# Weights prepared one product earlier: the order of weight casts, block factors and late loads in a two-layer mixer trunk

## The chip, the core and the metric

The kernel runs on one core of a Trainium2 chip. TensorE multiplies matrices, VectorE and ScalarE do elementwise work, GpSimd (POOL) and SyncE (SP) mostly issue DMAs here. The metric is the device time of one execution in microseconds.

## What is computed

Two layers over 2048 tokens of 1024 features. Cut to what matters:

```python
for l in range(2):
    shift, scale, gate = split(silu(c) @ w_ada[l] + b_ada[l], 3)
    h = rms_norm(x, g_pre[l]) * (1 + scale) + shift
    u_a, b_a, c_a, gate_a, u_p, gate_p = split(h @ w_in[l], 6)
    y_a = b_a * causal_conv3(c_a * u_a, w_conv[l]) * silu(gate_a)
    y_p = pool(u_p, w_pool[l], pool_scale[l]) * silu(gate_p)  # windows 2, 4, 8, 16
    y = concat([y_a, y_p]) @ w_out[l]
    x = x + gate * rms_norm(y, g_post[l])
```

All tensors are float32.

## The kernel before, in words

Features lie on the partitions, in chunks of 128 (k = 0 to 7); tokens go in two blocks of 1024, each in two halves of 512. Every float32 operand of a large product is split into a high part, rounded by a cast, and a low part, source less high part; a product is made of three passes (high·high, high·low, low·high), each a matmul of 128x128 weights with 128x512 data.

The work is a row of phases, for layer and block (0,0), (0,1), (1,0), (1,1): an in-phase (h times w_in, and the mixer, into y), then an out-phase (y times w_out, evicted to DRAM as ysp, with the sums of its squares), in which the operands h of the next block are also made. The block factor ry, one over the root of the mean square of y times w_out, comes after the out-phase, in the first stretch of the next in-phase: `opening(p)` evicts the last column chunk (p = 0), splits the sums of squares (`mean_split`, p = 1), and at p = 3 sums them over the partitions by two matmuls a half (`mean_mm`) and makes the factors: logarithm and exponential on ScalarE, each behind a load of its table, then three Newton steps on VectorE (L278 to L280). Tasks in the background (`Paced`) use ry to finish the block: ysp times ry, plus x, to x1 or to the output.

In layer 0 an in-phase takes 24 column groups with all 8 chunks each. In layer 1 `in_seven` multiplies by Winograd's form of Strassen's scheme: two column groups, two halves of k and two halves of the tokens form a 2x2 block product in 7 products of 12 matmuls instead of 8. Twelve pairs of column groups give 84 products. Four of the seven weight operands are sums, split beforehand and loaded from DRAM ready (512 KB, POOL's queue, L714); three are raw quarters (256 KB, SP's queue) that ScalarE casts (L729) and VectorE settles, that is subtracts for the low part (L739). They lie in a ring of seven slots. The sums of data blocks of h come from the out-phase, twelve "late" ones (L1038, split at L183 and L186) in the first products. After each product, ScalarE or VectorE takes its result from PSUM (L828 to L860).

```python
    LOAD, HIGH, SETTLE = 6, 3, 2
...
            for p, (_, hn) in enumerate(PRODUCTS):
                m = 7 * n + p
                load(m + 1 + LOAD)
...
                if final and p in closing:
                    free -= closing[p](kept)
                free -= settle(m + 1 + SETTLE)
                high(m + 1 + HIGH)
```

So weights are loaded six products ahead, cast three and settled two ahead. In the last pair `closing[p]` brings y back from DRAM (`yin`, loaded at L884 into six landing buffers) in 14 pieces of 128x512, splits them for the out-phase, and loads and settles the first weights of the out-phase, whose class `Weights` has the same three steps (cast L209, settle L219). In the in-phases and the out-phases those weights share three slots in turn.

Each engine runs its instructions in the order in which they stand in the program (`manual_schedule`), and so do the queues of SP and POOL: an instruction that waits holds all behind it on its engine. The places of tiles (`ring`, `wplaces`, `yorder`) are lists of slot numbers; a tile in a slot waits for the last reader of the tile that lay there.

## Time and profile before

| | |
|---|---|
| runs of the kernel | 1442.15, 1446.51, 1449.56 us, median 1446.51 |
| the profiled execution | 1441.82 us |
| its span in the trace | 1440.0 us |
| mean granted TensorE clock | 0.986 of full speed |
| in-phase (0,0) and start | to 318.4 us |
| out-phase, in-phase, out-phase of (0,0) to (0,1) | to 763.6 us |
| in-phase (1,0), 84 products | 763.6 to 1008.3 us |
| out-phase (1,0) | to 1095.5 us |
| in-phase (1,1), 84 products | to 1335.0 us |
| last out-phase | to the end |

How to read it: an engine's busy time counts only its own instructions, so TensorE at 97% leaves 48 us in which it stands. A row of the timeline gives the start, the time that the run of like instructions took, their number, and in brackets how long the engine stood before and which instruction released it. The granted clock is 1.00 at 2.4 GHz and 0.50 at 1.2 GHz.

### The profile page before, as it was taken

To read this page: it belongs to the slowest core of one execution; us is meant where nothing else is said; L and a number is where in the kernel's file an instruction comes from. 1 tells how busy PE (TensorE), PEld (TensorE's weight loads), DVE (VectorE), ACT (ScalarE), POOL (GpSimd) and SP (SyncE) were. 2 spreads that over 40 slices of the span, in tenths; PEclk is the share of its full clock that TensorE was granted. 3 is DMA by queue.
4 is the path that set the end of the run, shared out by engine and by line. 5 is a ranking of instruction groups with operands and counts; after the bars stand their busy time and mean duration, and the time that the engine had idled before them with its cause. 6 is when DMAs were issued, how large, how long until landed. Compare 5 with 4: busy or idle time off the path is not lost. (4 is left out here: it accounts for less than half of the span.)

```text
span 1440.0 us, 17843 instructions
## 1 busy us (share of the span) xinstructions
PE 1391.7 (97%) x6244; PEld 1142.8 (79%) x6244; DVE 932.5 (65%) x1519; ACT 500.9 (35%) x869; POOL 256.9 (18%) x372
## 2 busy tenths in 40 slices
PE   8889999999999999999997999999998999999996
PEld 4678888878888888888885888887886888887796
DVE  7962778755445575775855766768765655658455
ACT  4332334444443222224646222123645111113421
POOL 4601123310011111210121222210122122121000
PEclk9999999999999999999999999999999999999998
DMA  8405678635446656654567888887458677877422
GB/s 309 182 0 180 236 242 292 215 140 181 137 146 204 220 184 204 212 169 138 199 210 239 247 244 254 270 245 255 151 194 285 208 229 231 240 237 240 143 88 88
DMA packets 143116, 291.23 MB, mean 202 GB/s; under 512 B 15921, under 2 KB 32305, under 8 KB 143026
## 3 DMA queue, kind: packets, MB, share of 16 engines
q1 hardware_dynamic: 96338, 171.58, 36.4%
q0 software_dynamic: 46688, 118.51, 25.2%
q8 instruction: 49, 0.80, 0.2%
q14 instruction: 41, 0.34, 0.1%
HBM read 217.67 MB, written 72.35 MB: 201 GB/s over the span
## 5 line engine op out<-in xcount | busy, mean ns | idle before, releaser
L804 PE MATMUL ps_in<-h,ws 128*128 128x512 f32 x2016 | 464.6, 392 | 16.6 <-DVE ws L739 15.1
L804 PEld LDWEIGHTS ps_in<-h,ws 128*128 128x128 f32 x2016 | 379.9, 189 | 100.5 <-DVE ws L739 19.7
L390 PE MATMUL ps_in<-h,ws 128*128 128x512 f32 x1968 | 450.6, 390 | 0.0
L390 PEld LDWEIGHTS ps_in<-h,ws 128*128 128x128 f32 x1968 | 368.7, 188 | 76.0
L390 PE MATMUL ps_out<-y,ws 128*128 128x512 f32 (+1 forms) x1728 | 353.7, 367 | 2.2 <-ACT ws L209 2.0
L390 PEld LDWEIGHTS ps_out<-y,ws 128*128 128x128 f32 x1728 | 298.7, 189 | 56.6 <-ACT ws L209 2.9
L209 ACT CAST ws<-raw 128x512 fp32r<-128x512 f32 x146 | 89.6, 622 | 300.5 <-PE ps_in L390 144.9
L219 DVE TENSOR_TENSOR ws<-raw,ws 128x512 fp32r<-128x512 f32 x146 | 99.6, 688 | 115.8 <-ACT ws L209 112.8
L390 PE MATMUL ps_in<-h,w 128*128 128x512 f32 x336 | 86.8, 418 | 14.3 <-ACT h L379 7.2
L714 POOL DMA_DIRECT2D ws<-sums x96 | 67.5, 704 | 185.4 <-PE ps_in L804 171.8
L390 PEld LDWEIGHTS ps_in<-h,w 128*128 128x128 f32 x336 | 66.8, 201 | 33.6 <-ACT h L379 9.6
L987 POOL DMA_DIRECT2D ysp<-yg x48 | 26.1, 544 | 269.9 <-ACT yg L986 269.7
L828 ACT COPY v<-ps_in 128x512 f32<-128x512 f32 x24 | 14.1, 589 | 167.3 <-PE ps_in L804 167.3
L739 DVE TENSOR_TENSOR ws<-raw,ws 128x512 fp32r<-128x512 f32 x72 | 49.3, 685 | 17.6 <-ACT ws L729 17.6
L729 ACT CAST ws<-raw 128x512 fp32r<-128x512 f32 x72 | 41.5, 620 | 24.0 <-PE ps_out L390 17.7
L263 DVE SCALAR_TENSOR_TENSOR adaw<-adaw,cb 128x512 f32<-128x512 f32 x64 | 42.8, 685 | 10.7 <-DMA adaw<-wada 9.0
L849 ACT ACTIVATE second<-second 128x1024 f32<-128x1024 f32 x16 | 17.0, 1062 | 93.1 <-DVE second L843 90.2
L995 DVE TENSOR_TENSOR acc<-acc,sq 128x512 f32<-128x512 f32 x42 | 28.9, 692 | 24.9 <-ACT sq L992 24.9
L473 POOL DMA_DIRECT2D sums<-s13h x24 | 18.0, 748 | 147.3 <-ACT s13h L465 123.1
L843 DVE TENSOR_TENSOR second<-ps_in,v 128x512 f32<-128x512 f32 x16 | 11.1, 692 | 44.4 <-PE ps_in L804 44.4
L1083 POOL DMA_DIRECT2D x<-fin x32 | 18.8, 586 | 116.6 <-DVE fin L1078 113.8
L1076 DVE TENSOR_TENSOR fin<-fin,ry 128x512 f32<-128x512 f32 x48 | 32.8, 684 | 6.0 <-DMA fin<-ysp 6.0
(178 smaller groups left out, 1322.5 us busy)
## 6 DMA issues: line engine op xcount, KB each, us to landing
ws<-sums POOLq DMA_DIRECT2D x96, 512.0 KB, 7.1
raw<-win SPq DMA_DIRECT2D x122, 256.0 KB, 4.4
adaw<-wada SPq DMA_DIRECT2D x64, 256.0 KB, 4.5
raw<-wout SPq DMA_DIRECT2D x64, 256.0 KB, 3.3
sums<-raw POOLq DMA_DIRECT2D x48, 256.0 KB, 5.0
ysp<-yg POOLq DMA_DIRECT2D x48, 256.0 KB, 3.7
fin<-ysp SPq DMA_DIRECT2D x48, 256.0 KB, 4.9
raw<-win SPq DMA_DIRECT2D x80, 128.0 KB, 4.5
```

The lines of the kernel that those rows point to most:

```text
L209: nc.scalar.copy(self.ws[m][:, 0], self.raws[m].rearrange("p (a b) -> p a b", b=P))
L219: nc.vector.tensor_tensor(t[:, 1], raw, t[:, 0].bitcast(F32), op=ALU.subtract)
L263: nc.vector.scalar_tensor_tensor(w[n], w[n], 1.0, cb[:, n * HS : (n + 1) * HS], op0=ALU.mult, op1=ALU.mult, accum_out=m[:, l, j : j + 1])
L390: nc.tensor.matmul(ps[s], lhsT=ws[k // KH][:, wi, k % KH, :], rhs=rhs(k, ri, s), start=first and (wi, ri) == PASSES[0], stop=last and (wi, ...
L714: nc.gpsimd.dma_start(ops[m].rearrange("p a b c -> p a (b c)"), sums[l, n][:, :, SUM[a]])
L729: nc.scalar.copy(ops[m][:, 0], raws[m].rearrange("p (a b) -> p a b", b=P))
L739: nc.vector.tensor_tensor(ops[m][:, 1], raw, ops[m][:, 0].bitcast(F32), op=ALU.subtract)
L804: nc.tensor.matmul(ps, lhsT=ops[m][:, wi, k, :], rhs=h[hn][k][:, ri, :], start=p < 4 and k == 0 and (wi, ri) == (0, 0), stop=k == KH - 1 a ...
L987: nc.gpsimd.dma_start(ysp[l, b][:, j, s * HS : (s + 1) * HS], t)
L995: tt(accs[s], accs[s], q, op=ALU.add)
L1076: nc.vector.tensor_tensor(e[0], e[0], ry[l, b, s], op=ALU.mult)
L1083: nc.gpsimd.dma_start(x1[b][:, k, s * HS : (s + 1) * HS], e[1])
```

## The change

Six edits in the order of the work; no arithmetic is changed.

- `in_phase` takes the weights of the out-phase behind it (`nxt`) and casts, loads and settles the first of them between the matmuls of its last product; the background work is paced to end four steps sooner.
- In `in_seven` the settle and the cast stand right behind a product's matmuls, ahead of the opening, of the closing and of what takes the product's result; they are for products three and four ahead.
- The ring begins with the slots that come free first: `turned` and `wplaces[1:] ... wplaces[:1]`.
- `opening` sums the squares and begins both factors at p = 2, behind one table load that serves logarithm and exponential (`log_exp`, which moves from the head of the out-phase to its norm and to p = 2), and ends them at p = 3 and p = 4. There are 13 table loads in the program instead of 19.
- `closing` begins at the last product of the pair before the last and goes in threes: y is loaded two products before its split. The first out weights are loaded at p = 2 and p = 4 and settled at p = 3 and p = 4.
- `out_last` takes its weights' raw parts from the three buffers of `w`, not from the six landings, and casts before it loads, half by half.

```diff
-    def in_phase(l, b, hrhs, tasks, later, started, yplaces, wplaces, ws=None, opening=None):
+    def in_phase(l, b, hrhs, tasks, later, started, yplaces, wplaces, nxt, ws=None, opening=None):
...
                         ws.settle(2)
-        bg = Paced(tasks, 1, KT * (len(order) - first) - (10 if started else 20))
+        bg = Paced(tasks, 1, KT * (len(order) - first) - (10 if started else 24))
         for n in range(first, len(order)):
...
                 turn = KT * (n - first) + k
-                if opening and turn in (0, 4, 9):
-                    opening((0, 1, 3)[(0, 4, 9).index(turn)])
+                if n == len(order) - 1 and k > KH:
+                    if k == KH + 1:
+                        nxt.high(2)
+                        nxt.load(3)
+                    else:
+                        free -= nxt.settle(k - KH - 1)
+                if opening and turn in OPENING:
+                    opening(OPENING.index(turn))
                     free = 0
                 free = work.run(free)
-                if not opening or turn > 9:
+                if not opening or turn > OPENING[-1]:
                     bg.run(free + 1 if free > 0 else 0)
...
+    OPENING = (0, 4, 9, 11, 13)
+
     def in_weights(l, order, first, places):
...
     SUM = {"S1": 0, "S2": 1, "S3": 2, "S4": 3}
-    LOAD, HIGH, SETTLE = 6, 3, 2
+    LOAD, HIGH, SETTLE = 6, 4, 3
...
                 later.tick()
-                free = 2.5
+                free = 2.5 - settle(m + 1 + SETTLE)
+                high(m + 1 + HIGH)
                 if n == 0:
...
                         bg.prime(1)
-                if final and p in closing:
-                    free -= closing[p](kept)
-                free -= settle(m + 1 + SETTLE)
-                high(m + 1 + HIGH)
                 if p == 0:
...
                     free -= E2
+                at = p if final else p - 7 if n == len(PAIRS) - 2 else None
+                if at == -1:
+                    bg.drain()
+                if at in closing:
+                    free -= closing[at](kept)
                 free = mix.run(free)
-                if (n or p > 3) and n < len(PAIRS) - 1:
+                if (n or p > 4) and n < len(PAIRS) - 1 and at != -1:
                     bg.run(max(free, 0.1))
-                if n == len(PAIRS) - 2 and p == 6:
-                    bg.drain()
         mix.drain()
...
-        log_exp()
         h = {name: [None] * KH for name in EARLY + LATE}
...
         def norm():
+            log_exp()
             for s in range(NH):
...
                 st["parts"] = [mean_split(accs.pop(s)) for s in range(NH)]
-            if p == 3:
-                st["mean"] = [mean_mm(parts) for parts in st["parts"]]
+            if p == 2:
+                log_exp()
                 for s in range(NH):
-                    ry[l, b, s] = rsqrt_short(st["mean"][s], HS, half("ry"))
+                    ry[l, b, s] = half("ry")
+                    st[s] = rsqrt_steps(mean_mm(st["parts"][s]), HS, ry[l, b, s])
+                    next(st[s])
+            if p in (3, 4):
+                for _ in st[p - 3]:
+                    pass
...
             for j in range(KT):
-                if part == 0 and j:
-                    ws.load(2 * j + 6)
-                    ws.high(2 * j + 3)
                 ps = bank("ps_out")[:, :n]
                 for i, k in enumerate(OUT_ORDER if part or j == 0 else range(KT)):
+                    if part == 0 and i % KH == 0:
+                        ws.high(2 * j + i // KH + 3)
+                        ws.load(2 * j + i // KH + 5)
                     if part == 0 and i % KH == 1:
...
+    turned = lambda places, n: places[n % 3 :] + places[: n % 3]
+
     def between(many, few):
...
             tasks += [call_task(lambda: load_wpool(1), 0.1)]
-            y = in_phase(0, 0, hrhs, tasks, later, started, yplaces, wplaces)
+            ws = out_weights(0, turned(wplaces, 34))
+            y = in_phase(0, 0, hrhs, tasks, later, started, yplaces, wplaces, ws)
     with working(8, 6, 4, 3, 0), tc.manual_schedule():
-        ws = out_weights(0, wplaces)
-        ws.load(3)
-        ws.settle(2)
-        first = in_weights(0, IN_ORDER, 0, wplaces[1:] + wplaces[:1])
+        first = in_weights(0, IN_ORDER, 0, turned(ws.places, 16))
         hrhs, _, opening = out_phase(0, 0, y, 0, 1, ws, hplaces, None, first)
...
         tasks = between(mixes, fins[:4]) + between(between(adas, sums_), fins[4:])
-        y = in_phase(0, 1, hrhs, tasks, later, None, yplaces, first.places, first, opening)
+        ws = out_weights(0, first.places)
+        y = in_phase(0, 1, hrhs, tasks, later, None, yplaces, first.places, ws, first, opening)
     wplaces = first.places
     with working(5, 8, 6, 3, 2), tc.manual_schedule():
-        ws = out_weights(0, wplaces)
-        ws.load(3)
-        ws.settle(2)
         for n, (l, b) in enumerate(blocks[2:], 2):
...
             h, fills, opening = out_phase(*blocks[n - 1], y, l, b, ws, hplaces, lplaces)
-            ring = wplaces[:2] + yorder[:4] + wplaces[2:3]
+            ring = wplaces[1:] + yorder[:4] + wplaces[:1]
             hp = {}
...
             if last:
-                ws = out_weights(l, after + late_places[:9], lambda: landing("raw"))
+                ws = out_weights(l, after + late_places[:9])
             else:
...
                 def f(kept):
-                    if p == 0:
-                        for q in inner[:4]:
-                            y_load(*q)
-                        ws.load(1)
-                        return 0
-                    for q in inner[4 * p - 4 : 4 * p]:
+                    for q in inner[max(0, 3 * p - 3) : max(0, 3 * p)]:
                         y_settle(*q, kept)
-                    for q in inner[4 * p : 4 * p + 4]:
+                    for q in inner[3 * p + 3 : 3 * p + 6]:
                         y_load(*q)
-                    return 2.8 + (ws.settle(p - 2) if p > 2 else 0)
+                    if p == 2:
+                        ws.load(2)
+                    if p == 4:
+                        ws.load(3)
+                    return 2.1 * (p > 0) + (ws.settle(p - 2) if p in (3, 4) else 0)
...
-            closing = {p: close(p) for p in range(5)}
+            closing = {p: close(p) for p in range(-1, 6)}
             kept = in_seven(l, b, h, fills, opening, tasks, later, old, closing)
```

What it moves, at three places.

ScalarE at the opening of in-phase (1,0), before: `ws<-raw` is the cast of a weight, `ah` and `late` are the statistics' and the operands' high parts, `rs_a`, `rs_v`, `ry` the factors.

```order
L729 CAST ws<-raw 128x512 x2
L286 ACT_TABLE_LOAD
L286 ACTIVATE rs_a<-ps_stat,epsc 128x512
L287 ACTIVATE rs_v<-ps_stat,epsc 128x512
L288 ACT_TABLE_LOAD
L288 ACTIVATE ry<-rs_a 128x512
L286 ACT_TABLE_LOAD
L286 ACTIVATE rs_a<-ps_stat,epsc 128x512
L287 ACTIVATE rs_v<-ps_stat,epsc 128x512
L288 ACT_TABLE_LOAD
L288 ACTIVATE ry<-rs_a 128x512
L729 CAST ws<-raw 128x512
```

ScalarE at the same place, now, beginning at the copy of the first product's result:

```order
L833 COPY v<-ps_in 128x512
L737 CAST ws<-raw 128x512
L183 CAST h<-late 128x512 x4
L183 CAST ah<-acc 128x512 x2
L883 ACT_TABLE_LOAD
L286 ACTIVATE rs_a<-ps_stat,epsc 128x512
L287 ACTIVATE rs_v<-ps_stat,epsc 128x512
L288 ACTIVATE ry<-rs_a 128x512
L286 ACTIVATE rs_a<-ps_stat,epsc 128x512
L287 ACTIVATE rs_v<-ps_stat,epsc 128x512
L288 ACTIVATE ry<-rs_a 128x512
L737 CAST ws<-raw 128x512
```

The casts of the fifth and the sixth weight stood together right ahead of the table loads; the sixth's, the first cast here, now stands ahead of the last late operands, and the factors stand behind one table load instead of four.

VectorE at the same opening, before: `v` and `second` are what takes the products' results.

```order
L830 TENSOR_TENSOR v<-ps_in,v 128x512
L739 TENSOR_TENSOR ws<-raw,ws 128x512
L834 TENSOR_TENSOR second<-ps_in,v 128x512
L278 SCALAR_TENSOR_TENSOR rs_a<-rs_v,ry 128x512
L279 TENSOR_TENSOR rs_a<-rs_a,ry 128x512
L280 SCALAR_TENSOR_TENSOR ry<-rs_a,ry 128x512
L278 SCALAR_TENSOR_TENSOR rs_a<-rs_v,ry 128x512
L279 TENSOR_TENSOR rs_a<-rs_a,ry 128x512
L280 SCALAR_TENSOR_TENSOR ry<-rs_a,ry 128x512
L739 TENSOR_TENSOR ws<-raw,ws 128x512
L838 TENSOR_TENSOR second<-ps_in,second 128x512
```

VectorE there, now:

```order
L835 TENSOR_TENSOR v<-ps_in,v 128x512
L747 TENSOR_TENSOR ws<-raw,ws 128x512
L839 TENSOR_TENSOR second<-ps_in,v 128x512
L278 SCALAR_TENSOR_TENSOR rs_a<-rs_v,ry 128x512
L279 TENSOR_TENSOR rs_a<-rs_a,ry 128x512
L280 SCALAR_TENSOR_TENSOR ry<-rs_a,ry 128x512
L843 TENSOR_TENSOR second<-ps_in,second 128x512
L747 TENSOR_TENSOR ws<-raw,ws 128x512
L278 SCALAR_TENSOR_TENSOR rs_a<-rs_v,ry 128x512
L279 TENSOR_TENSOR rs_a<-rs_a,ry 128x512
L280 SCALAR_TENSOR_TENSOR ry<-rs_a,ry 128x512
```

The settle that stood behind both factors (L739) now stands ahead of them (the first L747 here), and another product's result is taken between the two.

VectorE in the last pair of products of a seven-product in-phase, before: `y<-yraw,y` splits y, L219 settles weights of the out-phase.

```order
L186 TENSOR_TENSOR y<-yraw,y 128x512 x4
L739 TENSOR_TENSOR ws<-raw,ws 128x512
L834 TENSOR_TENSOR second<-ps_in,v 128x512
L186 TENSOR_TENSOR y<-yraw,y 128x512 x4
L219 TENSOR_TENSOR ws<-raw,ws 128x512
L739 TENSOR_TENSOR ws<-raw,ws 128x512
L838 TENSOR_TENSOR second<-ps_in,second 128x512
L186 TENSOR_TENSOR y<-yraw,y 128x512 x2
L219 TENSOR_TENSOR ws<-raw,ws 128x512
L843 TENSOR_TENSOR second<-ps_in,v 128x512
L853 TENSOR_TENSOR cv<-ps_in,cv 128x512
L860 TENSOR_TENSOR v<-ps_in,v 128x512
```

VectorE there, now:

```order
L747 TENSOR_TENSOR ws<-raw,ws 128x512
L839 TENSOR_TENSOR second<-ps_in,v 128x512
L186 TENSOR_TENSOR y<-yraw,y 128x512 x3
L843 TENSOR_TENSOR second<-ps_in,second 128x512
L186 TENSOR_TENSOR y<-yraw,y 128x512 x3
L219 TENSOR_TENSOR ws<-raw,ws 128x512
L186 TENSOR_TENSOR y<-yraw,y 128x512 x3
L219 TENSOR_TENSOR ws<-raw,ws 128x512
L848 TENSOR_TENSOR second<-ps_in,v 128x512
L858 TENSOR_TENSOR cv<-ps_in,cv 128x512
L186 TENSOR_TENSOR y<-yraw,y 128x512 x2
L865 TENSOR_TENSOR v<-ps_in,v 128x512
```

The settles of the seven-product weights (L739, now L747) leave the rows between the y splits; the last accumulation (L860, now L865) has two more y splits right ahead of it and stands behind all fourteen.

## Rows read from the trace of the kernel before

**Rows 1.** The page: the span and the engines' busy times.

```profile
span 1440.0 us, 17843 instructions
PE 1391.7 (97%) x6244; PEld 1142.8 (79%) x6244; DVE 932.5 (65%) x1519; ACT 500.9 (35%) x869; POOL 256.9 (18%) x372
```

**Rows 2.** Sums of waits on TensorE: us in total, times, longest.

```profile
PE ps_in L804 <- DVE ws L739: 15.1, 8, 7.8
```

**Rows 3.** Timeline of TensorE: start, length, what, count, wait before and releaser.

```profile
318.38 1.20 PE L390 MATMUL ps_out<-y,ws 128*128 128x512 f32 x4 [1.45 <-ACT ws L209]
...
764.34 11.46 PE L804 MATMUL ps_in<-h,ws 128*128 128x512 f32 x48 [0.71 <-ACT ws L729]
...
788.80 110.20 PE L804 MATMUL ps_in<-h,ws 128*128 128x512 f32 x478 [7.81 <-DVE ws L739]
...
899.30 92.82 PE L804 MATMUL ps_in<-h,ws 128*128 128x512 f32 x408
...
1003.13 5.28 PE L804 MATMUL ps_in<-h,ws 128*128 128x512 f32 x22 [1.25 <-DVE ws L739]
...
1096.16 11.46 PE L804 MATMUL ps_in<-h,ws 128*128 128x512 f32 x48 [0.71 <-ACT ws L729]
...
1115.37 208.65 PE L804 MATMUL ps_in<-h,ws 128*128 128x512 f32 x912 [2.46 <-DVE ws L739]
...
1329.87 5.28 PE L804 MATMUL ps_in<-h,ws 128*128 128x512 f32 x22 [1.40 <-DVE ws L739]
1334.99 5.60 PE L390 MATMUL ps_out<-y,ws 128*128 128x512 f32 x24
1341.14 41.56 PE L390 MATMUL ps_out<-y,ws 128*128 128x512 f32 x192 [0.56 <-ACT ws L209]
```

**Rows 4.** Windows: PE, PEld, DVE, ACT, POOL busy (instructions), granted clock, DMA share, GB/s.

```profile
789.00:790.00 1.00, 1.00 (x3) 0.81 (x4) 1.00 (x3) 0.00 (x0) 0.00 (x0) 0.50 0.23 41
1003.00:1004.00 1.00, 0.87 (x4) 0.74 (x5) 1.00 (x3) 0.00 (x0) 0.00 (x0) 1.00 0.98 385
```

**Rows 5.** Timeline of ScalarE at the first opening.

```profile
776.87 1.28 ACT L286 ACT_TABLE_LOAD   x1
...
783.97 1.28 ACT L288 ACT_TABLE_LOAD   x1
785.27 0.63 ACT L288 ACTIVATE ry<-rs_a 128x512 f32<-128x512 f32 x1
```

**Rows 6.** Timeline of VectorE at the first opening.

```profile
775.42 1.29 DVE L186 TENSOR_TENSOR al<-acc,ah 128x512 fp32r<-128x512 f32 x2
...
785.93 0.69 DVE L278 SCALAR_TENSOR_TENSOR rs_a<-rs_v,ry 128x512 f32<-128x512 f32 x1 [2.37 <-ACT ry L288]
...
788.06 0.69 DVE L739 TENSOR_TENSOR ws<-raw,ws 128x512 fp32r<-128x512 f32 x1
```

**Rows 7.** POOL's timeline; then line L714, loads of ready sums.

```profile
758.50 0.71 POOL L714 DMA_DIRECT2D ws<-sums  x1 [1.23 <-PE ps_out L390]
...
DMA to landing us min/median/max: 4.1/7.1/12.4
```

**Rows 8.** Line L1038, loads of the late operands.

```profile
DMA to landing us min/median/max: 2.7/4.8/5.5
```

**Rows 9.** Timeline of VectorE in the second closing.

```profile
1324.67 0.68 DVE L739 TENSOR_TENSOR ws<-raw,ws 128x512 fp32r<-128x512 f32 x1
...
1335.19 0.69 DVE L860 TENSOR_TENSOR v<-ps_in,v 128x512 f32<-128x512 f32 x1 [1.43 <-PE ps_in L804]
```

**Rows 10.** Timeline of ScalarE in the second closing.

```profile
1315.44 0.59 ACT L828 COPY v<-ps_in 128x512 f32<-128x512 f32 x1 [16.89 <-PE ps_in L804]
```

**Rows 11.** The page's row on out weights; line L884, loads of y.

```profile
raw<-wout SPq DMA_DIRECT2D x64, 256.0 KB, 3.3
...
DMA to landing us min/median/max: 2.8/3.9/11.1
```

**Rows 12.** Timeline of VectorE in the out-phase (1,0).

```profile
1018.14 0.69 DVE L219 TENSOR_TENSOR ws<-raw,ws 128x512 fp32r<-128x512 f32 x1
```

## The prediction

> **What bounds the kernel now.** The page's first part comes first: TensorE is busy 97% of the span, so whatever is won must be won where it stands still or runs slowly [rows 1]. The sums of its waits come next: the largest releaser by far is VectorE's settle of a weight (L739), 15.1 us in 8 waits [rows 2]. Then TensorE's timeline shows where: not in the steady stretches, which run at one pace (408 matmuls in 92.82 us, 0.2275 us each; a product of twelve is 2.73 us), but at phase borders [rows 3]. There are four kinds: the border from the first in-phase to its out-phase (1.45 us at 318.38); the openings of the two seven-product phases (0.71 before the first product, 7.81 and, in the second, 2.46 before the sixth); their closings (1.25 and 1.40 before the last products); and the start of the last out-phase (0.56) [rows 3]. Behind the long stall the granted clock is 0.50 in the slice 789 to 790, that is 1.2 instead of 2.4 GHz, while it stays at 1.00 behind the stall of 1.25 us [rows 4]: a long stop costs twice.
>
> What the stops cost is counted as time less matmuls at 0.2275 us. Opening 1: 763.63 (764.34 less 0.71) to 899.30 is 135.7 us; the 540 matmuls (45 products) and six for statistics need 124.2; lost 11.5. Closing 1: 899.30 to the end of the row at 1003.13 (1008.4, whose last matmul is drawn some 0.2 long) against 470 matmuls, 106.9: lost 2.0. Opening 2: 1095.45 to 1324.02 against 978 matmuls, 222.5: lost 6.1. Closing 2: 1324.02 to 1334.99 against 34 matmuls, 7.7: lost 3.2. First border: 1.45, and 0.3 more in the four matmuls behind it: 1.8. Sum 24.6 us; the 0.56 at 1341.14 (0.7 so counted) stands apart.
>
> **The change part by part.**
> *Weights of the next phase in the last product of an in-phase.* The first two casts move ahead of the SiLU and the table load on ScalarE, their settles go with them; the third ring slot is free by then and the second is freed by the fourth step of that product. The raw loads stand on SP behind loads that are already done. TensorE's own work covers them: 1.8 us go, nothing replaces them.
>
> *Weights first, three products ahead.* At the sixth product of opening 1, TensorE waits for a settle (DVE, 788.06). That settle stands behind the Newton steps of both block factors; those of the second (785.93) wait for an exponential on ScalarE (785.27), the end of a chain with four table loads that begins at 776.87 [rows 5, 6]. In the new order that settle stands ahead of the factors (second piece of the order), and one table load serves instead of four (first piece), so the 7.81 us wait, its twin of 2.46 and both clock drops lose their cause. The 0.71 go too: the first weight takes the ring slot that the last out-phase freed 10.9 us (48 matmuls) before its end, so its cast no longer waits for the last matmul. Together 11.5 + 6.1 = 17.6 us; what is late next are two things.
> First, the second operand (a 512 KB load on POOL's queue) now takes the slot freed by the last-but-one weight half, 24 matmuls before the end. The row at 758.50 shows a load released by just that event, 5.1 us before 763.63; a load of this kind lands after 7.1 us in the median, 4.1 to 12.4 [rows 7]: at 765.6, while the second product begins at 766.4. Two more loads and the late operands are in the air at that time. From 0 to 4.5 us each time; I take 0.3 each, 0.6. The Trainium skill (DMA: Bandwidth & Descriptors, section "Anatomy of one DMA — SWDGE (gpsimd) path") puts such a DMA at 2.0 us plus bytes over 436 GB/s, by which I estimate 3.2 us for 512 KB and no wait at all here. The trace does not agree (7.1), so the 0.6 stays; by the page the total would be 0.6 lower.
> Second, the statistics matmuls stand after three products instead of four. They need the low part of the squares' sum, which VectorE finished at 776.71, 13.1 us after the border [rows 6]; now it is wanted after 8.2 us, at 771.8. It does come sooner, as the late operands' casts no longer queue behind a cast that waits for the border: six of the twelve landed long before, the eighth (issued at about 759, when the second is settled, with a landing of 4.8 to 5.5 [rows 8]) is there at some 764, and thirteen ScalarE instructions of about 0.6 us overlapped by a little and two settles later it is about 772.7. A wait of 0 to 2.5 each; I take 0.9 each, 1.8.
>
> *Block factor in small steps, one table load.* Six table loads fewer in all (19 to 13); those in the middle of the out-phase lie beside matmuls and cost nothing now. The factor's VectorE steps are cut in two, with the accumulation between; that is free while the sixth weight is already settled.
>
> *y two products ahead, the closing's settles behind the weights.* The waits of closings 1 and 2 come from y splits that stand ahead of the settles (DVE, 1324.67) [rows 9]; now the settles stand first (third piece of the order): 2.0 + 3.2 us go. What is late next is the end of the same queue. Before, the last accumulation (L860) ran 0.2 us after the phase's end, at 1335.19 [rows 9]. Now it stands behind fourteen y splits and both out weights, and the first out weight's load stands on SP behind twelve y loads, each of which waits for a landing buffer freed by a settle. Counted from the end of the first product at 1315.4 [rows 10]: the third ends at 1320.9; the second group of y is settled by 1323.8; the twelfth y load and then the weight's load are issued at 1324.1 and the weight lands 3.3 us later [rows 11], 1327.4; behind it the casts of three y, of the second weight and of the SiLU, with their splits; the accumulation at about 1334.7, when the phase ends at 1331.8. Its followers (0.7, 1.2, a cast, a split) bring the last y at 1338.6; the last out-phase wants it 1331.8 + 4.8 = 1336.6. That is 2.0 us, and 1.3 more for the table load (1.3 [rows 5]) and the cast of the third weight behind it; the 0.7 that stood there goes: 2.6 net, between -0.5 (weights land at once) and 5. In closing 1 the out-phase is twice as wide, so the last y is in time; but the third weight's settle (done at 1018.83 [rows 12], 10.6 us into the phase) is wanted 11.8 us in, and with the chain some 3 us later it misses that by about 1.9; 0 to 4.
> For this chain the Trainium skill (ScalarE: Activation LUTs, section "What ACT_TABLE_LOAD costs") adds 1.38 us of drain to the 1.28 of a load. The trace shows the next instruction at work 1.30 us after the load began (783.97, then the exponential at 785.27 [rows 5]), so it doesn't bear that out; by the page the last closing would lose about 1.4 us more.
>
> **Sum.** 24.6 - 0.6 - 1.8 - 1.9 - 2.6 = 17.7 us. The profiled execution took 1441.82 us, span and 1.8 around it; so 1424.1. The runs' median, 1446.51, is 4.7 above that execution; the same distance gives 1428.8. I predict 1428.
>
> **Rivals.**
> *All of it goes* (0.15): landings at the low end of their rows, no new wait. For it: the steady stretches show that this order of queues runs without a gap. Against: the closings' chain is in the order. 24.6 and the 0.7: 1446.5 - 25 = 1421.
> *The stalls move* (0.17): the new waits sit at the upper ends. 2 x 1.5 for the second operand, 2 x 2.5 for the statistics, 4 and 5 in the closings, 17 in all, so 7 to 8 stay and the time is 1439; more than that if a wait reaches 2.46 us, behind which the trace has the clock low. For it: y loads take up to 11.1 us to land when queues are full [rows 11].
> *Slower* (0.04): casts three products ahead come before the copy out of PSUM on ScalarE. If raws landed later than ScalarE reaches them, each would hold the copy, then VectorE, then the banks. There are 72 such casts; the waits must pass 25 us in sum to turn the sign, 0.35 us a cast; at 0.6 each it is 43 us and 1446.5 - 17.7 + 43 = 1472. Against it: the steady stretch shows no wait at a lead of two products, and loads stay six ahead.
> *It doesn't do what it says* (0.02): another wait stands just behind each one removed, so 1443 to 1447.
>
> **How the numbers follow.** The forecast has 0.62, with a range of its own from 1421 to 1435. The 0.5% (7.2 us) that a measurement of this kernel can tell from no change is 1439.3. Faster: 0.62 + 0.15 + 0.10 of the moved stalls = 0.87; within 0.5%: 0.07 of these and half of the last case, 0.08; slower: 0.05. The range 1419 to 1439 takes in both neighbours.
>
> **What would show it.** Right: no gap over 1 us at the sixth product of either seven-product phase and no slice at clock 0.50 behind it; no wait for L747 in the closings; small new gaps before the statistics matmuls, before the second product (releaser a DMA of sums), in the first 6 us of the last out-phase (releaser the last y or its weight) and some 12 us into the out-phase before it. Wrong: no gaps at those places (then 1421), or gaps of 2 us and more there; or ScalarE waiting for raw weights inside the steady stretches. The total is wrong in kind if TensorE's idle time falls by less than 10 us.

## The result, and the profile after

The changed kernel takes 1431.28 us (median of 6 runs, 1429.6 to 1431.91), the kernel before 1447.13 (6 runs, 1442.15 to 1449.56): a ratio of 0.9894, 95% interval 0.9874 to 0.9914. The forecast was 1428, 1419 to 1439.

The page of the changed kernel, its span and busy times, and of its fifth part (the costliest groups: what they worked, and what ended the engine's idle time before them) the two groups whose matmuls waited before [rows 1, 2]:

```profile
span 1429.8 us, 17848 instructions
PE 1389.4 (97%) x6244; PEld 1143.6 (80%) x6244; DVE 932.2 (65%) x1519; ACT 493.5 (35%) x863; POOL 257.7 (18%) x372
...
L812 PE MATMUL ps_in<-h,ws 128*128 128x512 f32 x2016 | 458.4, 389 | 0.4 <-DMA ws<-sums 0.4
...
L390 PE MATMUL ps_out<-y,ws 128*128 128x512 f32 (+1 forms) x1728 | 357.1, 368 | 7.0 <-DVE ws L219 2.9
```

The same row of the out-phases before:

```profile
L390 PE MATMUL ps_out<-y,ws 128*128 128x512 f32 (+1 forms) x1728 | 353.7, 367 | 2.2 <-ACT ws L209 2.0
```

The seven-product matmuls wait 0.4 us, where the settle alone made 15.1 [rows 2]; those of the out-phases wait 7.0 instead of 2.2. TensorE's timeline shows where:

```profile
317.73 87.20 PE L390 MATMUL ps_out<-y,ws 128*128 128x512 f32 x384
...
455.20 1.13 PE L416 MATMUL ps_wu<-wp,wupt 128*128 128x128 f32 x8 [1.72 <-DMA wupt<-wupt]
...
767.49 5.74 PE L812 MATMUL ps_in<-h,ws 128*128 128x512 f32 x24 [0.43 <-DMA ws<-sums]
...
774.38 117.18 PE L812 MATMUL ps_in<-h,ws 128*128 128x512 f32 x516
...
1010.46 77.15 PE L390 MATMUL ps_out<-y,ws 128*128 128x512 f32 x332 [2.75 <-DVE ws L219]
...
1096.89 0.50 PE L308 MATMUL ps_stat<-ah,ones 128*128 128x512 f32 x1 [1.12 <-ACT ah L183]
...
1327.29 0.50 PE L390 MATMUL ps_out<-y,ws 128*128 128x512 f32 x1 [2.90 <-ACT y L183]
...
1329.74 42.70 PE L390 MATMUL ps_out<-y,ws 128*128 128x512 f32 x192 [0.99 <-ACT ws L209]
```

The waits at the border of the first in-phase, at the sixth products and in the closings [rows 3] are gone. New are the waits that the forecast named (sums 0.43, statistics 1.12, third weight 2.75, last y 2.90), and one that it did not, for `wupt` in in-phase (0,1). Cut at the phases' first matmuls (before the two seven-product phases of the kernel before, 0.71 us earlier, where their wait begins), the two profiled executions compare so (us):

| phase | before | after | difference | forecast |
|---|---|---|---|---|
| start to end of out-phase (0,0) | 406.1 | 404.8 | -1.3 | -1.8 |
| in-phase (0,1) | 270.4 | 272.4 | +2.0 | 0 |
| out-phase (0,1) | 87.2 | 87.0 | -0.2 | 0 |
| in-phase (1,0) | 244.6 | 231.6 | -13.0 | -12.3 |
| out-phase (1,0) | 87.2 | 91.7 | +4.5 | +1.9 |
| in-phase (1,1) | 239.5 | 231.6 | -8.0 | -8.1 |
| last out-phase | 105.0 | 110.8 | +5.8 | +2.6 |
| span | 1440.0 | 1429.8 | -10.2 | -17.7 |

So the stalls went as forecast, and the new waits cost 7.8 us more (2.0, 2.6 and 3.2). The first line holds 0.8 us by which the start was slower in the later execution (out-phase (0,0) wanted at 317.73, before at 316.93); the border itself gave 2.1. The medians lie 15.9 apart and not 10.2, since the profiled execution of before was 5.3 us faster than its median and that of after (1431.54) was not.

### The profile page after: what moved, and what is told of

It reads as the page before. It is cut to its first block, busy times and chain, and to the rows that moved or that the text cites. A ratio compares the mean times of both kernels' runs of the same rounds, so it can differ in the third digit from the quotient of the medians.

```text
span 1429.8 us, 17848 instructions
## 1 busy us (share of the span) xinstructions
PE 1389.4 (97%) x6244; PEld 1143.6 (80%) x6244; DVE 932.2 (65%) x1519; ACT 493.5 (35%) x863; POOL 257.7 (18%) x372
## 4 chain that ended last, share of the span: by engine, by line
PE 88%; DVE 6%; DMA 3%; ACT 1%; issue 1%; SPq 0%; DVEq 0%; ACTq 0%
PE ps_in L390 34%; PE ps_in L812 29%; PE ps_out L390 23%; DVE ada L237 1%; PE ps_wu L416 1%; DVE x L378 1%; DMA late<-late 1%; DMA raw<-wout 1%; DMA wupt<-wupt 1%; DMA ws<-sums 1%; DVE y L186 1%; DVE h L382 1%; PE ps_stat L308 0%; PE ps_warm L1209 0%; DVE apre L1241 0%
## 5 line engine op out<-in xcount | busy, mean ns | idle before, releaser
L219 DVE TENSOR_TENSOR ws<-raw,ws 128x512 fp32r<-128x512 f32 x146 | 99.8, 688 | 131.5 <-ACT ws L209 131.5
L747 DVE TENSOR_TENSOR ws<-raw,ws 128x512 fp32r<-128x512 f32 x72 | 49.3, 685 | 0.0
L993 ACT ACTIVATE yg<-ps_out,gg 128x512 f32<-128x512 f32 x48 | 32.9, 686 | 11.8 <-PE ps_out L390 11.8
```

The costliest lines, as they stand in the source:

```text
L219: nc.vector.tensor_tensor(t[:, 1], raw, t[:, 0].bitcast(F32), op=ALU.subtract)
L747: nc.vector.tensor_tensor(ops[m][:, 1], raw, ops[m][:, 0].bitcast(F32), op=ALU.subtract)
L993: nc.scalar.activation(t, ps[s], AF.Copy, scale=gg[:, l, j : j + 1])
```

## The experiments

Ratios are to the kernel before, timed on the same chip. Three experiments are single runs without a ratio, and are marked so.

**The kernel before, a second profile** (a single run)

> The kernel before, unchanged, with a second profile. Its runs lie between 1442 and 1450 us, those of the changed kernel within 2.3 us. Theory: the spread comes from the openings' wait for a settle (7.81 in the first, 2.46 in the second, in the first profile), so that in a slower execution the second opening's wait is 4 us or more, and TensorE's clock falls behind it. Rival: the spread comes from the start phase (to 318 us), and both openings read as before, within 0.5 us.

1445.48 us, span 1443.7. The waits of the two openings:

```profile
778.70 0.51 PE L308 MATMUL ps_stat<-ah,ones 128*128 128x512 f32 x1 [1.10 <-ACT ah L183]
...
792.15 111.10 PE L804 MATMUL ps_in<-h,ws 128*128 128x512 f32 x478 [6.70 <-DVE ws L739]
...
1120.13 207.01 PE L804 MATMUL ps_in<-h,ws 128*128 128x512 f32 x912 [2.47 <-DVE ws L739]
```

The second opening waits 2.47 again, so the theory fell; the rival is half right, with 1.8 of the 3.7 us ahead of 407.9, but the first opening took 2.4 more (statistics 1.10 late, and slower matmuls behind 6.70). The second took less: its 912 matmuls 207.01 us, not 208.65 [rows 3].

**Casts and settles behind the opening again**

```diff
-    LOAD, HIGH, SETTLE = 6, 4, 3
+    LOAD, HIGH, SETTLE = 6, 3, 2
...
-                free = 2.5 - settle(m + 1 + SETTLE)
-                high(m + 1 + HIGH)
+                free = 2.5
...
                     if p == 2:
                         bg.prime(1)
+                free -= settle(m + 1 + SETTLE)
+                high(m + 1 + HIGH)
```

> The changed kernel, but casts and settles again stand behind the opening, and three and two products ahead. Theory 1 (as predicted: the order of weights against factors removed the openings' wait): 5 to 12 us slower than the changed kernel, with a wait for a settle at the sixth product of both openings. Theory 2 (the one table load and the split factor remove it just as well): within 2 us of the changed kernel, and at most 1 us of wait for a settle at each opening.

1433.44 us (ratio 0.9912, 0.9895 to 0.9929), 0.7 to 2.6 us above the changed kernel by the ratios, and no wait for a settle at either opening. Theory 2 holds; its 2 us lie inside that.

**Both factors whole, behind the fourth product**

```diff
-            if p == 2:
-                log_exp()
...
+            if p == 3:
+                st["mean"] = [mean_mm(parts) for parts in st["parts"]]
+                for s in range(NH):
+                    ry[l, b, s] = rsqrt_short(st["mean"][s], HS, half("ry"))
```

> The changed kernel, but the statistics' matmuls and both block factors stand whole behind the fourth product (four table loads again). Theory 1 (the order of the weights suffices): 0 to 2 us faster than the changed kernel, since the statistics' matmuls come one product later and wait for nothing (1.12 and 0.31 us go at the second opening). Theory 2 (the small steps are needed): 8 to 14 us slower, with waits for a settle or a free bank behind the factors.

1433.2 us (0.9914, 0.9898 to 0.9931). By the ratios that is 1.0 to 2.9 us above the changed kernel, so neither time came: theory 1 had 0 to 2 us less, theory 2 had 8 to 14 more. The statistics wait for nothing, as theory 1 says. The expectation was wrong on one more point: there is no table load ahead of the factors here, because `log_exp` stays in the out-phase's norm and its table stays in place. New waits for a bank of PSUM stand behind the factors, and are small, 0.84 at the first opening and at the second:

```profile
1107.82 212.50 PE L812 MATMUL ps_in<-h,ws 128*128 128x512 f32 x936 [1.35 <-DVE second L843]
```

**Both of these edits undone**

> The changed kernel with both edits of the openings undone: casts and settles behind the opening at a lead of three and two, and both factors whole behind the fourth product. Each alone cost 2 us. Theory (either edit alone keeps the sixth weight's settle ahead of TensorE, so their worth shows only when both are gone): a wait for a settle of 6 to 8 us at the first opening and 2 to 3 at the second, 8 to 13 us slower than the changed kernel, 1439 to 1444. Rival (the two costs add up, and the 7.81 us went by another edit, the ring or the late operands): 3 to 5 us slower, 1434 to 1436, no wait over 2 us.

1442.88 us (0.9976, 0.9963 to 0.9989): 10.9 us above the changed kernel beside it (1431.99, below), as the theory had it. TensorE's timeline again:

```profile
784.68 113.66 PE L812 MATMUL ps_in<-h,ws 128*128 128x512 f32 x490 [4.26 <-DVE ws L747]
...
1114.16 216.19 PE L812 MATMUL ps_in<-h,ws 128*128 128x512 f32 x946 [3.31 <-DVE ws L747]
```

The settles' wait is back at both, though 4.26 at the first and not 7.81. Either edit alone keeps the settle ahead of TensorE; a test that undoes one shows each as worth 1 to 3 us. The missing 3.5 are the subject of the next run.

**The kernel before with the table load moved alone** (`log_exp` from the out-phase's head to its norm)

```diff
-        log_exp()
         h = {name: [None] * KH for name in EARLY + LATE}
...
         def norm():
+            log_exp()
             for s in range(NH):
```

> The kernel before, with one edit of the change alone: log_exp stands in the out-phase's norm and no longer at its head. With that the order has no table load at the first opening (four before), and the factors stay whole behind the fourth product. Theory (the four loads, 5.1 us, made most of the difference between the wait of 7.81 us at the first opening and that of 2.46 at the second, which has no table load before its factors): the first falls to 2 to 4.3 us, the slow clock behind it shortens, the second stays; 4 to 7 us faster than before, 1439 to 1442. Rival (the wait is Newton steps and queues, and the loads lay beside them): the first wait stays above 6 us, within 2 us of before.

1439.86 us (0.9963, 0.9947 to 0.9978), 5.8 us faster than before for one line, as the theory had it:

```profile
784.93 110.29 PE L804 MATMUL ps_in<-h,ws 128*128 128x512 f32 x478 [3.56 <-DVE ws L739]
...
1112.47 208.62 PE L804 MATMUL ps_in<-h,ws 128*128 128x512 f32 x912 [2.48 <-DVE ws L739]
```

7.81 became 3.56, 2.46 stayed. In the kernel before, ScalarE at the end of in-phase (0,1) shows why:

```profile
671.35 1.28 ACT L875 ACT_TABLE_LOAD   x1
672.63 1.28 ACT L599 ACT_TABLE_LOAD   x1
```

L875 is the load of `log_exp`, L599 the in-phase's last SiLU. The load stood ahead of that SiLU, which put its own table in again, so that four loads followed at the opening [rows 5].

**The ring in its old order** (a single run)

```diff
-            ring = wplaces[1:] + yorder[:4] + wplaces[:1]
+            ring = wplaces[:2] + yorder[:4] + wplaces[2:3]
```

> The changed kernel with the ring of slots in its old order. Theory (the slot decides): the first cast of both seven-product phases waits for the last out-phase's matmuls again, 0.7 us before the first product, and the load of sums for the second product waits no longer than before, 0 instead of about 0.4; so within 1 us of the changed kernel. Rival (the place of the cast in the queue decides, not the slot): no wait before the first product.

1443.63 us, 12 more than the changed kernel. The wait of 0.7 came as the theory had it, its "within 1 us" did not. ScalarE at the first opening, TensorE at both, and one window (columns as in [rows 4]):

```profile
763.50 0.62 ACT L737 CAST ws<-raw 128x512 fp32r<-128x512 f32 x1 [8.86 <-PE ps_out L390]
...
774.62 1.17 ACT L183 CAST ah<-acc 128x512 fp32r<-128x512 f32 x2
```

```profile
764.17 8.74 PE L812 MATMUL ps_in<-h,ws 128*128 128x512 f32 x36 [0.71 <-ACT ws L737]
775.32 0.80 PE L308 MATMUL ps_stat<-ah,ones 128*128 128x512 f32 x1 [2.41 <-ACT ah L183]
...
1106.34 0.80 PE L308 MATMUL ps_stat<-ah,ones 128*128 128x512 f32 x1 [3.00 <-ACT ah L183]
```

```profile
776.00:780.00 4.00, 3.73 (x10) 2.85 (x10) 3.66 (x7) 3.87 (x6) 0.00 (x0) 0.50 1.16 391
```

The cast that waits 8.86 us for the last matmuls holds on ScalarE the late operands behind it and the cast `ah`, which runs at 774.62 instead of 771.96. The statistics, now behind three products, wait for it, and the clock falls to 1.2 GHz (granted 0.50 from 776 to 780). The openings lose 6.7 and 7.0 us (133.7 us against 558 matmuls, 237.2 against 1012) where the changed kernel loses 0.7 and 1.3. Of the 17.6 that they lost in the kernel before, 13.7 are there again, so the earlier statistics need the ring's new order.

**The next weights not in the in-phase's last product** (a single run)

```diff
-                if n == len(order) - 1 and k > KH:
...
+        ws.load(3)
+        ws.settle(2)
         first = in_weights(0, IN_ORDER, 0, turned(ws.places, 16))
```

> The changed kernel, but the first out weights are loaded, cast and settled at the start of the out-phases in layer 0, as before. Theory: 1.45 and 0.16 us of wait at the border from the first in-phase to its out-phase come back, and nothing at the second such border: 1.6 us slower than the changed kernel. Rival (the table load that was moved out of the way gave it): under 0.5 us of wait at that border.

1432.86 us. TensorE and ScalarE at the first border:

```profile
318.32 87.20 PE L390 MATMUL ps_out<-y,ws 128*128 128x512 f32 x384
```

```profile
307.79 0.62 ACT L209 CAST ws<-raw 128x512 fp32r<-128x512 f32 x1
313.08 0.62 ACT L209 CAST ws<-raw 128x512 fp32r<-128x512 f32 x1 [4.68 <-PE ps_in L390]
318.30 1.09 ACT L599 ACTIVATE sga<-ps_in 128x512 f32<-128x512 f32 x2 [4.59 <-PE ps_in L390]
```

No wait, as the rival said: the casts stand ahead of the SiLU (L599) without this edit. What is left at that border are the slots' turn (`turned`) and the place of `log_exp`, and the experiment with the table load moved alone tells them apart. TensorE, then ScalarE, in that run:

```profile
318.78 1.20 PE L390 MATMUL ps_out<-y,ws 128*128 128x512 f32 x4 [1.45 <-ACT ws L209]
```

```profile
317.13 1.08 ACT L599 ACTIVATE sga<-ps_in 128x512 f32<-128x512 f32 x2 [10.60 <-PE ps_in L390]
318.11 1.66 ACT L209 CAST ws<-raw 128x512 fp32r<-128x512 f32 x3
```

With `log_exp` moved and the slots as before, the casts stay behind the SiLU and the 1.45 stay. So the slots' turn is needed; it was not run alone. In the text of the program without the edit the casts stand behind that SiLU, and yet its trace has them ahead of it: at this border the order on ScalarE is not that of the text.

**The out weights' loads ahead of y**

```diff
+                    if p in (0, 1):
+                        ws.load(p + 1)
                     for q in inner[3 * p + 3 : 3 * p + 6]:
                         y_load(*q)
-                    if p == 2:
-                        ws.load(2)
```

> The changed kernel, but in the closings the loads of the first two out weights stand ahead of the y loads of their step (steps 0 and 1 instead of 2). Theory (the first out weight's landing holds ScalarE for 4.5 us in both closings, and all behind it): the wait of 2.75 us in out-phase (1,0) goes with the slow clock behind it, 4.4 us, and of the 5.7 us at the start of the last out-phase 2 to 4 go: 6 to 8 us faster than the changed kernel, 1423 to 1426. Rival (the last accumulation is late because it stands behind fourteen y splits, and y lands late): under 2 us faster, and ScalarE waits for y loads in place of the weight.

1421.59 us (0.9835, 0.9816 to 0.9855), 9.7 less than the changed kernel's first median (8.5 to 10.4 by the ratios to before), more than the theory's 6 to 8. First the changed kernel's second closing, SP, then ScalarE, then VectorE:

```profile
1311.57 0.90 SPq L200 DMA_DIRECT2D raw<-wout  x2
```

```profile
1316.66 0.62 ACT L209 CAST ws<-raw 128x512 fp32r<-128x512 f32 x1 [4.34 <-DMA raw<-wout]
```

```profile
1317.31 0.69 DVE L219 TENSOR_TENSOR ws<-raw,ws 128x512 fp32r<-128x512 f32 x1 [3.73 <-ACT ws L209]
...
1323.86 0.69 DVE L865 TENSOR_TENSOR v<-ps_in,v 128x512 f32<-128x512 f32 x1
...
1327.27 1.29 DVE L186 TENSOR_TENSOR y<-cv,y 128x512 fp32r<-128x512 f32 x2 [0.74 <-ACT y L183]
```

The weight's load is issued at 1311.57 and lands 5.1 us later; ScalarE stands 4.34 for it and VectorE 3.73, so the last accumulation comes 4.9 us after the phase's end (1319.0), the last y at 1328.6. In the first closing it is the same: issued at 987.98, cast at 992.91. With the loads ahead, ScalarE, VectorE and TensorE:

```profile
1309.76 0.61 ACT L209 CAST ws<-raw 128x512 fp32r<-128x512 f32 x1
```

```profile
1317.68 0.68 DVE L865 TENSOR_TENSOR v<-ps_in,v 128x512 f32<-128x512 f32 x1
```

```profile
998.46 87.20 PE L390 MATMUL ps_out<-y,ws 128*128 128x512 f32 x384
...
1323.56 41.53 PE L390 MATMUL ps_out<-y,ws 128*128 128x512 f32 x192 [0.99 <-ACT ws L209]
```

The cast does not wait, the accumulation comes 1.0 us after the phase's end (1316.6), out-phase (1,0) takes 87.2 us again; of the last one's 5.8 a wait of 0.99 is left.

Two more readings bear on this. How long a weight takes to land there could be read before the change: the out weights that the kernel before issued between 970 and 1000, two of them, among the y loads of its first closing, give

```profile
DMA to landing us min/median/max: 5.3/7.8/10.4
```

And the wait in out-phase (1,0) has one more link. The changed kernel casts the third weight at 1003.91, but its settle stands on VectorE behind the first steps of the next block's norm, which wait for ScalarE:

```profile
1007.66 0.69 DVE L278 SCALAR_TENSOR_TENSOR rs_a<-rs_v,rn 128x512 f32<-128x512 f32 x1 [2.84 <-ACT rn L288]
...
1009.72 0.68 DVE L219 TENSOR_TENSOR ws<-raw,ws 128x512 fp32r<-128x512 f32 x1
```

The kernel before has the same order and is in time [rows 12]. Whether the settle ahead of the norm would remove the wait as well was not tried.

**The closing's plan of before, in fours**

```diff
-                    for q in inner[max(0, 3 * p - 3) : max(0, 3 * p)]:
...
+                    for q in inner[4 * p - 4 : 4 * p]:
                         y_settle(*q, kept)
...
-            closing = {p: close(p) for p in range(-1, 6)}
+            closing = {p: close(p) for p in range(5)}
```

> The changed kernel with the closing's plan of before: y in fours, loaded one product before its split, the first out weight's load behind the first four y loads; the settles of the seven-product weights stay ahead. Theory 1 (the settles' place took away the closings' waits, y's lead is worth nothing, and the early weight load is what the changed plan lost): like the kernel with the out weights first, 1421 to 1425, no wait over 1 us in out-phase (1,0). Theory 2 (y needs its two products): ScalarE waits for y loads, the accumulations behind them are late, and it is no faster than the changed kernel, 1429 to 1434.

1423.85 us (0.9851, 0.9838 to 0.9865): theory 1 holds, 8.1 us less than the changed kernel beside it. Out-phase (1,0) does not wait:

```profile
998.65 87.20 PE L390 MATMUL ps_out<-y,ws 128*128 128x512 f32 x384
```

The settles' place took the closings' waits away; y's longer lead brought nothing that these runs can tell, and its plan put the weight's load late.

**The background sooner**

```diff
-                if not opening or turn > OPENING[-1]:
+                if not opening or turn > 9:
...
-        bg = Paced(tasks, 1, KT * (len(order) - first) - (10 if started else 24))
+        bg = Paced(tasks, 1, KT * (len(order) - first) - (10 if started else 20))
```

> The changed kernel, but the background work of in-phase (0,1) begins behind the tenth group of matmuls again, not the fourteenth, with the old pacing. Theory (the wait of 1.72 us for a load of wupt in that phase comes from the mix tasks' new places, where one stands only twelve matmuls behind the last and its load waits for a landing buffer): that wait is under 0.3 us and the phase takes 270.4 us instead of 272.4; 1.5 to 2 us faster. Rival (it is a chance of that execution): 0 within 0.7 us, and the phase as long as before.

1428.32 us (0.9884, 0.9868 to 0.9899).

```profile
403.97 13.77 PE L390 MATMUL ps_in<-h,ws 128*128 128x512 f32 x60
...
674.35 87.20 PE L390 MATMUL ps_out<-y,ws 128*128 128x512 f32 x384
...
1008.28 75.56 PE L390 MATMUL ps_out<-y,ws 128*128 128x512 f32 x332 [2.95 <-DVE ws L219]
```

The phase runs from 403.97 to 674.35, 270.4 us, without the wait for `wupt` in between, so the background's later beginning and its pacing made the 2.0. The median is 3.7 below that of the changed kernel beside it. In the profiled execution, the fastest of its four, the 332 matmuls behind the wait of 2.95 took 75.56 us instead of 77.15, since the clock did not fall; whether that makes the other 1.7 of the median is not shown.

**The changed kernel again**

> The changed kernel again, on the chip of the other three: 1429 to 1433 us. A second profile of it shows the same waits at the same places: about 0.4 us for a load of sums and 0 to 1.5 for statistics at the openings, 2.5 to 3 us for a settle twelve us into out-phase (1,0), 2.5 to 3 for the last y in the last out-phase. Rival: they are chances of one execution and move by more than 1 us.

1431.99 us (0.9907, 0.9892 to 0.9922). The two large waits stand, one of them above its expected 3; the small ones move by up to 1.1 us (sums 0.43 to none, statistics 1.12 to none), so there the rival is right:

```profile
1010.79 78.11 PE L390 MATMUL ps_out<-y,ws 128*128 128x512 f32 x332 [3.48 <-DVE ws L219]
...
1327.43 1.95 PE L390 MATMUL ps_out<-y,ws 128*128 128x512 f32 x3 [2.89 <-ACT y L183]
```

**Three mended together**: weights ahead of y, background sooner, and

```diff
         n0 = b * TB
-        log_exp()
...
+                if part == 0 and j == 2:
+                    log_exp()
                 ps = bank("ps_out")[:, :n]
```

> The changed kernel with the out weights' loads ahead of y, the background work of in-phase (0,1) beginning behind the tenth group again, and the table load of the last out-phase moved behind its second chunk (0.99 us of wait for the cast of the third weight stood behind it). Theory (three separate waits, so their worth adds): 1421.6 less 2 for the mix tasks less 1 for the table load, 1417 to 1420; no wait for wupt in in-phase (0,1), none for a cast at the start of the last out-phase. Rival (one gives way to the next): 1421 to 1423.

1419.85 us (0.9815, 0.9802 to 0.9829), at the upper end of the expected sum and the lowest median of all, 11 to 13 us less than the changed kernel by the ratios. At the start of the last out-phase a wait of 0.22 and another of 0.22 for y's low part are left, no wait for a cast of a weight:

```profile
1318.09 0.50 PE L390 MATMUL ps_out<-y,ws 128*128 128x512 f32 x1 [0.22 <-ACT y L183]
```

Not undone in any run: the sixth edit, the raw buffers and the half-by-half casts of `out_last`.

## Why the prediction was right, and where not

- **The stalls that go: right in place and size.** In-phase (1,0) gave 13.0 (forecast 12.3), (1,1) 8.0 (8.1). The clock stays at 1.00 through both openings: the 516 matmuls at 774.38 take 117.18 us, 0.2271 each, the 972 behind the second opening's statistics 220.52 us.
- **Their cause: told too simply.** "In the new order that settle stands ahead of the factors" suffices where the table loads are gone, and is not necessary; the smaller steps do as well. And the four table loads were a cause of their own: taking them away in the kernel before gave 5.8 us by itself.
- **The ring: mechanism right, price wrong.** The forecast gave it 0.71 a phase, yet it said that the statistics come sooner because no cast waits at the border. Through that dependence the ring's order is worth some 12 us with the new opening, by a single run.
- **The first border: right order, wrong cause.** The casts moved ahead of the SiLU and the wait went (2.1 us, 1.8 forecast), but not by the edit in the last product: the turn of the slots did it, as far as the runs tell.
- **New waits at the openings: right.** Sums 0.43 and 0 (0.3 each forecast), statistics about 0.3 and 1.4 (0.9 each). The load of sums took 7.4 us in the median, 7.1 before [rows 7]. The Trainium skill (DMA: Bandwidth & Descriptors, "Anatomy of one DMA — SWDGE (gpsimd) path") gives 3.2 by my estimate; the trace does not agree.
- **New waits of the closings: the step that failed by its size.** The chain was named link by link and is there; out-phase (1,0) lost 4.5 (1.9 forecast, 0 to 4 its bounds), the last one 5.8 (2.6, -0.5 to 5), both beyond their bounds. By the forecast's own signs (gaps of 2 us and more there) this part was wrong. Counted from the end of the first product, the weight's load was issued when the forecast said (8.7 us). Two terms were too small. The weight was given 3.3 us to land, the median of its row [rows 11], in a stretch full of y loads where it took some 5 (4.9 and 5.1). The trace of before had this in view, with 5.3 and 10.4 us in its first closing. And a fall of the clock, named in a rival for waits of 2.46 us, has no term in the sum: the 332 matmuls behind the 2.75 took 77.15 us, 1.6 more than at 0.2275, the 192 behind the last wait 42.70 instead of 41.56 [rows 3]. A late first link is paid in every link behind it.
- **Not foreseen: +2.0 in in-phase (0,1).** The background there begins later and is paced otherwise; undoing this takes the wait for `wupt` away. That the load lacked a free landing buffer fits the trace, but is argued. The forecast had no term for this phase.
- **From one execution to the median: wrong, and in the other direction.** From execution to execution the forecast was 1424.1 and 1431.5 came, 7.4 apart. TensorE's idle time fell by 7.9 us (48.3 to 40.4, span less busy time), less than the 10 below which the forecast calls its total wrong in kind. The added 4.7, by which before's median lay above its profile, does not belong to the kernel after, whose six runs lie within 2.3 us (five more within 5.3). Part of that scatter was in the first opening (2.4 of the 3.7 us between the two profiles of before), which the change took out. The two errors, 7.4 and 4.7, mostly cancel; the total came 3 us off by luck. (The sum itself gives 1428.8; 1428 was put down.)

## What to carry to other kernels

When a load is moved in a queue, ask what has to land before it can be issued: a weight needed first, issued behind twelve transfers that wait for buffers, cost more (9.7 us, by the run with the loads ahead) than the stalls that the change removed there (5.2). Take a load's landing time from the stretch where it will stand, not from the median of all. Edits that keep the same instruction from being late cover for one another: undo them singly and in pairs before calling one of them worthless. And before a forecast made from one execution is carried over to a median, ask whether the stalls that scatter are still there.

## What was not expected of the hardware

The clock fell behind some short waits, and the length of the wait does not tell which. Behind the wait of 2.75 us in out-phase (1,0), which TensorE entered after steady work, the next stretch of 4 us shows 0.75, a mix of the levels 2.4 and 1.2 GHz. In the run with the background sooner, the wait at the same place was longer, 2.95 us, and the clock stayed at 1.00. The changed kernel first, then that run:

```profile
1010.00:1014.00 4.00, 3.54 (x11) 2.86 (x12) 3.93 (x6) 0.00 (x0) 0.00 (x0) 0.75 0.65 197
```

```profile
1008.00:1012.00 4.00, 3.72 (x16) 3.10 (x17) 3.93 (x7) 0.00 (x0) 0.00 (x0) 1.00 0.65 211
```

The kernel before shows the same at its second opening: behind 2.46 us the clock fell in the first profile, behind 2.47 us it stayed at 1.00 in the second.

```profile
1117.40:1118.40 1.00, 1.00 (x4) 0.81 (x3) 0.00 (x0) 0.00 (x0) 0.00 (x0) 0.50 0.24 78
```

```profile
1120.00:1124.00 4.00, 3.87 (x17) 3.22 (x18) 2.56 (x5) 0.55 (x1) 0.00 (x0) 1.00 0.41 140
```

Behind 1.25 us it had stayed at 1.00 [rows 4]. So a wait of 2.5 to 3 us may cost its own length alone, or 1.6 us more (912 matmuls in 208.65 or 207.01 us, 332 in 77.15 or 75.56), in executions of the same or nearly the same program. What decides it, these runs do not show.
